# A two-layer decoder trunk on one core: when the first heads' transposes, the bias tables and the sevens' weights take their turn

## The chip, the core and the metric

The kernel runs on one core of one Trainium2 chip. TensorE multiplies matrices; VectorE, ScalarE and GpSimd do the element-wise work, each in the order of its own queue; DMA engines move data between HBM and the on-chip memories. The profile calls these engines PE (and PEld for the loading of its stationary operand), DVE, ACT and POOL; SP issues most DMAs. The metric is the time of one execution on the device in microseconds.

## The reference

Two layers over 256 tokens of width 2048, in float32. Each layer:

```python
h = rmsnorm(x)
q, k, v, gate_b, gate_c, conv_in = split(h @ w_in)     # six parts of 1024 columns
q, k = rmsnorm of q and k per head half (64 wide), with gains
A = (softmax(q0 k0 + bias) - lam * softmax(q1 k1 + bias)) @ v     # 8 heads, causal
A = rmsnorm(A per head) * (1 - lam_init)
conv = gate_b * causal_conv3(gate_c * conv_in)
x = x + concat(A, conv) @ w_out
x = x + relu(rmsnorm(x) @ w_up) ** 2 @ w_down          # width 8192
```

The bias depends on the distance between two tokens alone: a table of 32 buckets by 16 half-heads is turned into rows by distance, and each row is read as a Toeplitz band.

## The kernel before

**Precision and weights.** Every float32 operand is split into a high half in TensorE's fp32r format and a low half that holds the rest; a product takes three matmuls (high by high, high by low, low by high). Weights come in as tiles `raw` of 512 KB, four buffers deep, through SP's queue. `Weights.halves` converts an ordinary tile: ScalarE writes the high half `whi` (L335), VectorE subtracts it to get the low half `wlo` (L336). These two have three buffers each, so a tile is converted as soon as TensorE is done with the tile three places ahead of it. `Weights.take` issues the conversions three tiles ahead.

**Sevens.** Some pairs of the inner dimension are multiplied by Strassen's scheme with seven products instead of eight (`BySeven`). Such a pair needs two raw tiles. Its job `plain` converts the left tile into `w7b` and a half of the right one into `whi` and `wlo` (ScalarE L844, VectorE L845); `sums` builds two differences on VectorE (L877, L878), converts them into `w7x`, and builds two more (L882, L883); `more` converts these into `w7y`. The activations' sums (`sv`, `sf`) are made by `sums_of`. In the first projection (`first`) query and key of heads 0 to 3 are accumulated with one such pair in layer 0 and two in layer 1. In `left`, the first half of the output projection, pairs by seven ("a" and "b", L902) alternate with columns of gate_b ("c", L426). A column accumulates in the one PSUM bank of tag `av`; `gate` copies it out on ScalarE (L798), multiplies it with the convolution on VectorE, and converts the result.

**Order of the work.** TensorE's instructions run in program order. The other engines' order is planned at compile time from the data that each instruction needs and a model of the durations; `late` holds an instruction at its place in the program. Work beside the projections is written as generators in a list (`Background`, `work`). After every six matmuls of a projection (one k tile of 128 rows by two token tiles by three terms) `work.tick()` advances each of them that is due: `yield n` means n ticks later. In `linear_t` a tick comes more often.

What runs there, in layer 0: `load_bias`, due at tick 10, first runs `small_setup`: a matmul makes the rows by distance (L250), VectorE copies them out, a DMA on POOL's queue writes them to DRAM (L252); four ticks later the gains and lambda are prepared. Then two DMAs on POOL's queue read the band tables `rev` of 1 MB each (L284), and 12 ticks later ScalarE copies them, reversed, into `bias` (L293, eight copies over four steps, each held `late`). `Norm.factors` sums the squares of the rows (tot, L575); `rstd_of` computes the factor on POOL (row_e, row_r; L494, L496); a matmul spreads it (rbc).

`qk_norm` starts when a half's query or key is complete: squares on ScalarE (L645), sums on VectorE, the power on POOL, and the scaled heads on VectorE (L653). 12 ticks later come the transposes of the first 128 tokens, four on TensorE (L662), and one tick later those of the other 128. Each group of four is put away by two copies on ScalarE and two subtractions on VectorE for queries (`qT`, L619 and L621), and by four copies and two subtractions for keys (`kT`, L631 and L632; `kL`, L634). In the first half queries and keys are normalised in place. With 16 ticks to a projection, the queries' transposes of the first half stand after the 10th and 11th step of v's projection, the keys' after the 12th and 13th.

`attention` starts one tick after v's projection in the first half and ten in the second. Its four heads start 8 ticks apart (16 in the second half): copies of the query (`both`, L681), two ticks on the scores (L691, L694), bias and maximum on VectorE (L699), exponentials on ScalarE (L708); ten ticks later the transposes (`ptp`, L724), four ticks later the product with v (L735, L737), its copy (`ao`, L740) and its squares (L743). After the last head the norm, 12 ticks, and the transposes `atp` (L767). After the two halves' projections follow gate_c and conv_in (`gc`, `ci`, L474), then `left` and `right`, then the MLP, which the change does not touch.

Of the kernel before, what the change touches and what calls it, by code (L numbers as in the profile page):

```python
# [131 lines left out]
def trunk(ctx: ExitStack, tc: tile.TileContext, x, w_in, w_out, conv_w, q_norm_g, k_norm_g,  # L132
# [114 lines left out]
    def small_setup(vec, lamv, sel, rel, prod, by_dist):  # L247
# [27 lines left out]

    def load_bias(l, bpool, biasp, bias, setup):

        if l == 0:
            yield from small_setup(*setup)
        revs = []  # L280
        for j in range(2):
            rev = bpool.tile([P, NH, S], F32, tag="b", name=f"rev{l}{j}")
            src = by_dist_d[j * NH:(j + 1) * NH, 0:S]
            nc.gpsimd.dma_start(  # L284
                rev, bass.AP(src.tensor, src.offset, [[1, P], [REL, NH], [1, S]]))
            revs.append(rev)
        yield 4 if l else 12
        while held:
            yield 1
        bias += [biasp.tile([P, NH, S], F32, tag="bias", name=f"bias{j}") for j in range(2)]  # L290
        for h in range(0, NH, 2):
            for j in range(2):
                late(nc.scalar.activation(bias[j][:, h:h + 2],  # L293
                                          revs[j][:, h:h + 2, ::-1], AF.Copy))
            yield 2
# [24 lines left out]
    class Weights:  # L320
# [8 lines left out]
        def halves(self, raw):  # L329
# [4 lines left out]
            if not self.by_tile:  # L334
                pair = (nc.scalar.activation(hi, raw, AF.Copy),  # L335
                        nc.vector.tensor_sub(lo, raw, hi.bitcast(F32)))  # L336
                if self.ramp and len(self.made) < 7:
                    for ins in pair:
                        late(ins)
# [151 lines left out]
    def rstd_of(ss, n, name, shape):  # L491
# [3 lines left out]
        r = small.tile([P, shape], F32, tag="rs_r", name=f"{name}_r")  # L495
        nc.gpsimd.tensor_tensor(r, e, mhalf[:, :shape], op=ALU.pow)  # L496
        return r

    class Norm:
# [3 lines left out]
        def __init__(self, which, l):  # L503
            self.which, self.l = which, l
            self.squared = 0
            self.tiles = [Parts(apool, "a", f"nT{which}{l}_{n}") for n in range(D // CH)]
# [64 lines left out]
        def factors(self):  # L571
# [3 lines left out]
            nc.vector.tensor_reduce(tot, self.ss, axis=AX.X, op=ALU.add)  # L575
            r = rstd_of(tot, D, "row", NT)
            self.r = small.tile([P, NT], F32, tag="rowf", name="rowf", bufs=2)
# [60 lines left out]

    def qk_norm(acc, r, put, gain, name, in_place=False):

        out_ = []
        for t in range(NT):
# [5 lines left out]
                                    axis=AX.X, op=ALU.add)  # L648
            f = rstd_of(ms, DK, f"{name}{t}", NH)
            f2 = small.tile([P, NH], F32, tag="f2", name=f"{name}f{t}")  # L650
# [6 lines left out]
            out_.append(qn)  # L657
        yield 12
        for t in range(NT):
# [3 lines left out]
            put(tp.rearrange("p (h c) -> p h c", c=P), gain, slice(t * P, (t + 1) * P))  # L663
            yield 1

    def attention(l, qT, kT, kL, v, h0, dst, bias, tmp, pace, sums_of):
# [9 lines left out]
        def unit(i):  # L676
# [72 lines left out]
            for _ in range(2):  # L749
                nc.gpsimd.tensor_tensor(flat, flat, rflat, op=ALU.mult)  # L750
            f = rstd_of(flat, P, f"a{h0}", 4 * NT)
            f2 = small.tile([P, 4, NT], F32, tag="af2", name=f"af2{h0}", bufs=2)
# [42 lines left out]
    def gate(c, acc, cv, dst, y):  # L795

        ev = nat.tile([P, 2, S], F32, tag="wide", name=f"gb{c}")
        nc.scalar.activation(ev, acc, AF.Copy)  # L798
        nc.vector.tensor_add(y, ev[:, 0], ev[:, 1])
# [4 lines left out]
        dst.ready = c % KG == KG - 1  # L804


# [3 lines left out]
    class BySeven:  # L810
# [3 lines left out]
        def __init__(self, l, bpool, biasp, tmp, weights, rooms_of=4):  # L814
            self.rooms_of = rooms_of
            self.l, self.pool, self.weights = l, bpool, weights
            self.biasp, self.tmp = biasp, tmp
            self.sums, self.rooms = {}, []

# [19 lines left out]
        def jobs(self, w, i, cols, in_keys=False):  # L839

            mine = {}

            def split(hi, lo, src):
# [12 lines left out]
            def plain():  # L856
# [9 lines left out]
                room = self.pool.tile([P, 2, 2, CH], F32R, tag="b", name="w7b")  # L866
                b11, b21 = two(room, raws[0])
                hi = wpool.tile([P, 2, CH], F32R, tag="hi", name="whi")
                lo = wpool.tile([P, 2, CH], F32R, tag="lo", name="wlo")
                return b11, b21, split(hi[:, 0], lo[:, 0], raws[1][:, 1])  # L870

            def sums():
# [3 lines left out]

                nc.vector.tensor_sub(t[:, 0], right[:, 0], left[:, 0])  # L877
                nc.vector.tensor_sub(t[:, 1], right[:, 1], right[:, 0])  # L878
                room = self.biasp.tile([P, 2, 2, CH], F32R, tag="bias", name="w7x")
# [79 lines left out]
        def left(self, acts, cv):  # L959
# [8 lines left out]
            def column(c):  # L968
# [161 lines left out]
    def mixer(l, norm, loads):  # L1130

        with ExitStack() as scope:
# [24 lines left out]
            bias = []  # L1157
            work.start(load_bias(l, bpool, biasp, bias, setup), 20 if l else 10)
            hT = norm.tiles
# [5 lines left out]
            for half in range(2):  # L1165
# [19 lines left out]
                for t in range(NT):  # L1185
# [516 lines left out]
```

## Time and profile before

| | us |
|---|---|
| median of three runs (lowest, highest) | 2119.78 (2117.97, 2120.92) |
| the profiled execution | 2118.42 |
| its span, first to last instruction | 2116.6 |
| busy in the span: TensorE | 2107.7 |
| VectorE | 1817.5 |
| ScalarE | 1402.7 |
| POOL | 161.5 |

The granted clock of TensorE is 1.000 of full speed over the span. In a row of the timeline or of the chain of waits the first number is the start in microseconds from the span's first instruction, the second the duration; then engine, line, operation, output <- inputs, shapes and count; in brackets stands the idle time of the engine before the instruction and what ended it. In a row of waits stand the total, the number of times and the longest. A matmul's own duration overlaps its neighbours'; the distance between starts is what it costs.

### The profile page before, as it was taken

Reading aid. Unit: us, or ns where it says so; the run is one execution under the profiler, and the core shown is the slowest. Engines: PE = TensorE matmul, PEld = TensorE weight load, DVE = VectorE, ACT = ScalarE, POOL = GpSimd, SP = SyncE. Lnnn points to the kernel's source line nnn. Section 1 sums busy time; section 2 is a strip of 40 time slices with the busy share of each in tenths; the row PEclk is TensorE's granted clock in tenths of the full one; section 3 lists DMA queues with packets and bytes.
Section 4 is the critical chain, followed back from the end, with each engine's and each line's share of the span. In section 5 each row is a group of like instructions: output and inputs, shape, how many; then the busy total and the mean of one; then the engine's idle time right before and its main releaser. Section 6 shows DMA issues by size and latency. Waiting matters only on the chain.

```text
span 2116.6 us, 29201 instructions
## 1 busy us (share of the span) xinstructions
PE 2107.7 (100%) x10815; PEld 1800.4 (85%) x10815; DVE 1817.5 (86%) x2497; ACT 1402.7 (66%) x1817; POOL 161.5 (8%) x226
## 2 busy tenths in 40 slices
PE   9999999999999999999999999999999999999999
PEld 7888888888888888888888888888888888888887
DVE  7778788898888888799887788888988888888998
ACT  6777656676666676666567766557677677675664
POOL 2110100000000000011102101000000000000110
PEclk9999999999999999999999999999999999999999
DMA  7555565877777777789565555658877777777993
GB/s 272 178 159 172 179 207 189 288 253 225 234 232 230 233 232 230 247 298 311 171 219 170 163 174 181 200 180 295 259 230 234 231 231 235 230 231 256 318 309 111
DMA packets 312608, 476.01 MB, mean 225 GB/s; under 512 B 12724, under 2 KB 209670, under 8 KB 312465
## 3 DMA queue, kind: packets, MB, share of 16 engines
q1 hardware_dynamic: 284752, 406.76, 60.5%
q0 software_dynamic: 27520, 67.24, 10.1%
q8 instruction: 85, 1.39, 0.3%
q14 instruction: 59, 0.48, 0.1%
q10 hardware_dynamic: 192, 0.15, 0.0%
HBM read 440.52 MB, written 33.58 MB: 224 GB/s over the span
## 4 chain that ended last, share of the span: by engine, by line
PE 97%; ACT 1%; DMA 1%; DVE 1%; issue 0%; POOL 0%; ACTq 0%; DVEq 0%; POOLq 0%
PE upc L1376 31%; PE pr L1419 14%; PE dn L1500 8%; PE ci L474 4%; PE gc L474 4%; PE gb L426 4%; PE v L449 3%; PE o L919 3%; PE dn L1419 3%; PE k L449 2%; PE po L902 2%; PE q L449 2%; PE dn L1594 2%; PE pr1r L1419 2%; PE pr0r L1419 2%; PE po L919 2%
## 5 line engine op out<-in xcount | busy, mean ns | idle before, releaser
L1376 PE MATMUL upc<-nT,uhi 128*128 128x512 f32 x1920 | 454.7, 389 | 0.0
L1376 PEld LDWEIGHTS upc<-nT,uhi 128*128 128x128 f32 x1920 | 360.3, 188 | 74.7
L1241 DVE TENSOR_TENSOR ulo<-uraw,uhi 128x1024 fp32r<-128x1024 f32 x256 | 312.2, 1222 | 109.6 <-ACT f L1408 91.5
L335 ACT ACTIVATE whi<-raw 128x1024 fp32r<-128x1024 f32 x236 | 249.2, 1059 | 191.1 <-issue 20.6
L1240 ACT ACTIVATE uhi<-uraw 128x1024 fp32r<-128x1024 f32 x256 | 270.6, 1057 | 135.2 <-PE upc L1376 114.9
L336 DVE TENSOR_TENSOR wlo<-raw,whi 128x1024 fp32r<-128x1024 f32 x236 | 285.8, 1221 | 85.1 <-ACT whi L335 52.7
L1376 PEld LDWEIGHTS upc<-nT,ulo 128*128 128x128 f32 x1920 | 246.2, 191 | 9.4
L1376 PE MATMUL upc<-nT,ulo 128*128 128x256 f32 x1920 | 249.1, 283 | 0.0
L1266 ACT ACTIVATE bh<-draw 128x1536 fp32r<-128x1536 f32 x86 | 128.4, 1493 | 103.7 <-PE pr L1419 80.7
L1267 DVE TENSOR_TENSOR bl<-draw,bh 128x1536 fp32r<-128x1536 f32 x86 | 151.3, 1759 | 11.5 <-ACT bh L1266 11.0
L1500 PE MATMUL dn<-whi,fb 128*128 128x512 f32 x480 | 152.2, 389 | 0.0
L1419 PE MATMUL pr<-bh,f 128*128 128x512 f32 x360 | 121.4, 391 | 0.0
L335 ACT ACTIVATE whi<-uraw 128x1024 fp32r<-128x1024 f32 x60 | 63.7, 1062 | 71.9 <-PE dn L1500 55.1
L1386 ACT ACTIVATE ev<-upc 128x512 f32<-128x512 f32 x120 | 71.9, 599 | 54.2 <-PE upc L1376 54.2
L1266 ACT ACTIVATE t24h<-t 128x1024 fp32r<-128x1024 f32 x86 | 91.4, 1063 | 23.4 <-PE pr L1419 15.9
L1500 PEld LDWEIGHTS dn<-whi,fb 128*128 128x128 f32 x480 | 90.1, 188 | 18.8
L1267 DVE TENSOR_TENSOR t24l<-t,t24h 128x1024 fp32r<-128x1024 f32 x86 | 104.8, 1219 | 0.2
L1279 DVE TENSOR_TENSOR t<-draw 128x1024 f32<-128x1024 f32 x86 | 104.8, 1219 | 0.1
L1267 DVE TENSOR_TENSOR t13l<-t,t13h 128x1024 fp32r<-128x1024 f32 x86 | 104.8, 1219 | 0.0
L1266 ACT ACTIVATE t13h<-t 128x1024 fp32r<-128x1024 f32 x86 | 91.5, 1064 | 8.3 <-DVE t L1279 2.9
L1419 PE MATMUL pr<-t13h,f 128*128 128x512 f32 x240 | 93.8, 391 | 0.0
L1500 PE MATMUL dn<-wlo,fb 128*128 128x512 f32 x240 | 93.4, 389 | 0.0
(524 smaller groups left out, 4330.0 us busy)
## 6 DMA issues: line engine op xcount, KB each, us to landing
uraw<-in_w_up_dram SPq DMA_DIRECT2D x128, 1024.0 KB, 6.2
raw<-in_w_in_dram SPq DMA_DIRECT2D x191, 512.0 KB, 4.1
draw<-in_w_down_dram SPq DMA_DIRECT2D x180, 512.0 KB, 5.3
raw<-in_w_out_dram SPq DMA_DIRECT2D x64, 512.0 KB, 4.4
uraw<-in_w_down_dram SPq DMA_DIRECT2D x60, 512.0 KB, 6.6
hid0p<-f POOLq DMA_DIRECT2D x17, 512.0 KB, 3.5
fb<-hid0p POOLq DMA_DIRECT2D x17, 512.0 KB, 7.5
hid1p<-f POOLq DMA_DIRECT2D x17, 512.0 KB, 3.5
```

The source lines that it names most:

```text
L335: pair = (nc.scalar.activation(hi, raw, AF.Copy), nc.vector.tensor_sub(lo, raw, hi.bitcast(F32)))
L336: nc.vector.tensor_sub(lo, raw, hi.bitcast(F32)))
L449: nc.tensor.matmul(acc[:, t], a.ap[:, pa, k % KG, t * P:(t + 1) * P], (hi, lo)[pw][:, j], start=(k == 0 and (pa, pw) == (0, 0)), stop=(k = ...
L474: nc.tensor.matmul(acc[:, f, 0] if part else acc[:, f], wt[:, k % 4, fs], a.ap[:, 0, k % KG] if part else a.ap[:, :, k % KG], start=(part ...
L919: nc.tensor.matmul(accs[t], a.ap[:, pa, k % KG, t * P:(t + 1) * P], (hi, lo)[pw][:, j], start=(j == 0 and (pa, pw) == (0, 0) and (n, t) in ...
L1240: pair = (nc.scalar.activation(hi, src, AF.Copy), nc.vector.tensor_sub(lo, src, hi.bitcast(F32)))
L1241: nc.vector.tensor_sub(lo, src, hi.bitcast(F32)))
L1266: keep(nc.scalar.activation(hi, src, AF.Copy))
L1267: keep(nc.vector.tensor_sub(lo, src, hi.bitcast(F32)))
L1376: nc.tensor.matmul(acc[:, 0] if part else acc, wt[part][:, k], a.ap[:, 0, k % KG] if part else a.ap[:, :, k % KG], start=(part == 0 and kh ...
L1419: nc.tensor.matmul(prods[n], f[:, pa, a], b[pw], start=(start and m == 0), stop=(stop and m == 2))
L1500: nc.tensor.matmul(prods[p], f[:, pa, 2 * k + t], b[pw][:, n], start=(p in starts and k == 0 and m == 0), stop=(stop and k == 1 and m == 2))
```

## The change

It has three parts; no instruction that computes is added or taken away.

- *Bias tables.* The DMA that writes the rows by distance moves out of `small_setup` into `load_bias`. It is issued 8 ticks after the end of `small_setup`, once the row norm's power has been written into the program and no seven of the first projection is open, and `tc.issue_after` orders it behind that power on POOL's queue. The reads of the tables and, 12 ticks later, their copies move with it (from ticks 26 to 32 to ticks 35 to 41). In layer 1, nothing of this changes.
- *Transposes.* `qk_norm` takes its two delays as arguments. In the first half the queries wait 8 ticks instead of 12 and the keys 14; the two groups of each are 3 ticks apart instead of 1. They now stand after v's 6th and 9th step, and after its 14th and one step into the next projection. The first half's attention starts 4 ticks after v instead of 1; the second half's start is kept at 10.
- *Sevens.* `tc.issue_after(x)` orders, on the engine of x, each instruction of its block behind x. In `left`, the conversions of `plain` and the two differences of `sums` are ordered behind the last ordinary tile's conversion (ScalarE and VectorE) and the last gate copy (ScalarE) that precede them in the program. In the first projection this holds for the two differences alone, behind the last ordinary tile's low half.

```diff
-        nc.gpsimd.dma_start(by_dist_d, by_dist)
...
-    def load_bias(l, bpool, biasp, bias, setup):
+    def load_bias(l, norm, bpool, biasp, bias, setup):
         if l == 0:
             yield from small_setup(*setup)
+            yield 8
+            while norm.powered is None or held:
+                yield 1
+            with tc.issue_after(norm.powered.ins):
+                nc.gpsimd.dma_start(by_dist_d, setup[-1])
         revs = []
...
-    def qk_norm(acc, r, put, gain, name, in_place=False):
+    def qk_norm(acc, r, put, gain, name, in_place=False, wait=12, apart=1):
...
-        yield 12
+        yield wait
...
             put(tp.rearrange("p (h c) -> p h c", c=P), gain, slice(t * P, (t + 1) * P))
-            yield 1
+            yield apart
...
+            @contextmanager
+            def behind(ordered):
+                with ExitStack() as both:
+                    if ordered:
+                        for ins in self.weights.last + self.gated:
+                            both.enter_context(tc.issue_after(ins.ins))
+                    yield
...
-                b11, b21 = two(room, raws[0])
+                with behind(in_keys):
+                    b11, b21 = two(room, raws[0])
...
-                return b11, b21, split(hi[:, 0], lo[:, 0], raws[1][:, 1])
+                with behind(in_keys):
+                    b22 = split(hi[:, 0], lo[:, 0], raws[1][:, 1])
+                return b11, b21, b22
...
-                nc.vector.tensor_sub(t[:, 0], right[:, 0], left[:, 0])
-                nc.vector.tensor_sub(t[:, 1], right[:, 1], right[:, 0])
+                with behind(in_keys or self.rooms_of == 8):
+                    nc.vector.tensor_sub(t[:, 0], right[:, 0], left[:, 0])
+                    nc.vector.tensor_sub(t[:, 1], right[:, 1], right[:, 0])
...
-                gate(c, acc, cv, self.cat[2 + c // KG], y[:, c % 2])
+                self.gated = gate(c, acc, cv, self.cat[2 + c // KG], y[:, c % 2])
...
                     work.start(qk_norm(acc, norm.r, put, gain[:, l:l + 1], "qk"[n] + f"{l}{half}",
-                                       half == 0))
+                                       half == 0, *(((8, 3), (14, 3))[n] if half == 0 else (12, 1))))
...
                 work.start(attention(l, qT, kT, kL, v, h0, cat[half], bias[half], tmp,
-                                     1 + half, by_seven.sums_of), 1 + 9 * half)
+                                     1 + half, by_seven.sums_of), 4 + 6 * half)
```

The other lines of the diff set what these use: `Weights.last` is the last ordinary tile's pair of conversions, `gate` returns its copy, `rstd_of` returns its power, `Norm.powered` keeps it.

More of the change, by code (lines that the diff above doesn't have):

```diff
@@ L1 @@
 import math
-from contextlib import ExitStack
+from contextlib import ExitStack, contextmanager
 import concourse.bass as bass
@@ L336, in halves @@
                         nc.vector.tensor_sub(lo, raw, hi.bitcast(F32)))
+                self.last = pair
                 if self.ramp and len(self.made) < 7:
@@ L1157, in mixer @@
             bias = []
-            work.start(load_bias(l, bpool, biasp, bias, setup), 20 if l else 10)
+            work.start(load_bias(l, norm, bpool, biasp, bias, setup), 20 if l else 10)
             hT = norm.tiles
```

17 lines of the change are left out of this document (9 added, 8 removed).

## The prediction

> **What bounds the kernel now.** I read the first section of the page, then TensorE's own waits, then the timeline and the chain of waits around each of them. The execution that was profiled took 2118.42 us, 1.8 us of them outside its span.
>
> ```profile
> span 2116.6 us, 29201 instructions
> PE 2107.7 (100%) x10815; PEld 1800.4 (85%) x10815; DVE 1817.5 (86%) x2497; ACT 1402.7 (66%) x1817; POOL 161.5 (8%) x226
> ```
>
> TensorE is busy for all but 8.9 us, and the change removes no matmul. So it can win only what TensorE now loses in stalls. Its waits name them:
>
> ```profile
> PE q L449 <- DVE wlo L336: 2.1, 2, 1.1
> ...
> PE k L919 <- DVE wlo L336: 0.7, 1, 0.7
> ...
> PE po0r L902 <- DVE w7y L845: 0.3, 1, 0.3
> PE gb L426 <- ACT gb L798: 0.2, 1, 0.2
> ```
>
> Idle time understates a stall, because the pipeline has to fill again. The timeline of TensorE shows by how much, and shows one stall that has no idle time:
>
> ```profile
> 35.98 0.39 PE L919 MATMUL k<-whi,nT 128*128 128x512 f32 x1
> 37.07 0.50 PE L919 MATMUL k<-wlo,nT 128*128 128x512 f32 x1 [0.70 <-DVE wlo L336]
> 37.41 0.62 PE L919 MATMUL k<-whi,nT 128*128 128x512 f32 x2
> ...
> 39.70 1.17 PE L902 MATMUL po0r<-w7b,nT 128*128 128x512 f32 x3
> 40.71 0.86 PE L902 MATMUL q<-w7b,nT 128*128 128x512 f32 x3
> ```
>
> ```profile
> 56.60 12.24 PE v L449 x54
> ```
>
> Undisturbed, a matmul follows the last after 12.24 / 54 = 0.227 us, and six of them, one **step** of the background work, take 1.36 us. In the first fence the starts are 1.09 and 0.34 apart: 0.86 + 0.11 = 0.97 us lost for 0.70 shown, so 0.27 more than is shown. The three matmuls from 39.70 take 1.01 instead of 0.68: 0.33 lost, none of it shown. With 0.27 added to each wait, the stalls that the change can reach are 0.97 and 0.33 and 0.3 + 0.27 = 0.57 in the first projection of layer 0; 2.1 + 2 x 0.27 = 2.64 in the second half's query projection, one stall in each layer; 0.2 + 0.27 = 0.47 in a gate column. **Sum 4.98 us, 0.235%.** This is the most that the change can win; a measurement of this kernel tells about 0.2%, 4.2 us, from no change.
>
> **Part 1, the bias tables and the first product by seven.** The chain of waits there:
>
> ```profile
> 26.41 8.07 DMA raw<-in_w_in_dram
> ...
> 35.20 0.69 DVE w7t L878
> 35.88 1.14 DVE wlo L336
> ...
> 42.02 0.73 POOL row_r L496
> ```
>
> ```profile
> 34.59 0.69 DVE L877 TENSOR_TENSOR w7t<-raw 128x512 f32<-128x512 f32 x1 [3.71 <-DMA raw<-in_w_in_dram]
> ```
>
> ```profile
> L336 DVE TENSOR_TENSOR wlo<-raw,whi 128x1024 fp32r<-128x1024 f32 x236 | 285.8, 1221 | 85.1 <-ACT whi L335 52.7
> ...
> raw<-in_w_in_dram SPq DMA_DIRECT2D x191, 512.0 KB, 4.1
> ```
>
> ```profile
> 26.52 1.81 POOL L284 DMA_DIRECT2D rev<-by_dist_d  x2 [1.62 <-DMA by_dist_d<-setup]
> ```
>
> A load that takes 4.1 us elsewhere took 8.07, because both table reads of 1 MB were issued 0.1 us behind it. VectorE sat 3.71 us in front of two subtractions that need this load, while the ordinary tile's low half (35.88) stood behind them in its queue. The change removes both causes. The low half now goes first, into the idle 3.71 us that begin at 30.9; it needs 1.22 us and ends by 33 instead of 37.0, so the 0.97 stall goes. The load lands about 4 us earlier, at 30.5, so the subtractions follow at once, and VectorE's chain to the last parts of the seven (two adds of 0.69, three subtractions of 1.22) runs some 2 us sooner: it was late by 0.33 and 0.57. Nothing is added but order. I take all 1.87 us; if the row norm on POOL holds the last part, 0.57 stays.
>
> What the moved step issues: a small write and two reads on POOL's queue, now behind the pow at 42.02, so near 43 to 45. POOL's next work behind them is the query norm, after the projection has ended. Their readers and their new neighbours:
>
> ```profile
> rev<-by_dist_d POOLq DMA_DIRECT2D x2, 1024.0 KB, 10.0
> ```
>
> ```profile
> 51.20 1.06 ACT L335 ACTIVATE whi<-raw 128x1024 fp32r<-128x1024 f32 x1 [1.65 <-PE k L919]
> 52.16 1.14 ACT L293 ACTIVATE bias<-rev 128x512 f32<-128x512 f32 x2
> ```
>
> The reads take 10.0 us and land by 56. The copies of the tables, eight on ScalarE in pairs of 1.14 us, move from around v's start to its 5th to 11th step, from 56.6 + 5 x 1.36 - 1.9 = 61.5 on: over 5 us of cover. The Trainium skill, page "DMA: Bandwidth & Descriptors", Rules for kernel authors, says the reverse of this edit: issue a DMA early and wait late. In the trace the early issue cost 4 us on a load that TensorE needed, so here the row speaks against the rule; what the rule would make of the time is a rival below. The loads that the reads now meet are those of v's weights. The conversion at 51.20 waited for TensorE, not for its load; from it to v's first matmul (56.60) are 5.4 us, less 1.06 and 1.22 of conversion 3.1: its lead. A load that doubles as the one at 26.41 did is 4 us late. The loads are issued some 2 us sooner, as the sevens' buffers are returned sooner, so I take 0; bounds 0 and 1.
>
> ScalarE's room for the moved copies (the columns of busy time are PE, PEld, DVE, ACT, POOL):
>
> ```profile
> 62.00:86.00 24.00, 22.94 (x110) 18.67 (x109) 18.67 (x25) 18.11 (x24) 5.63 (x6) 1.00 0.50 151
> ```
>
> It is busy for 18.1 of these 24 us; three pairs move in, 3.4 us. It fits, and nearly fills it.
>
> **Part 2, the transposes.** ScalarE in front of the stall in layer 0:
>
> ```profile
> 74.79 1.04 ACT L335 ACTIVATE whi<-raw 128x1024 fp32r<-128x1024 f32 x1
> ...
> 76.30 0.68 ACT L631 ACTIVATE kT<-k00tp,gains 64x512 fp32r<-64x512 f32 x1
> ...
> 81.18 0.69 ACT L632 ACTIVATE kT<-k00tp,gains 64x512 fp32r<-64x512 f32 x1
> 81.89 2.01 ACT L335 ACTIVATE whi<-raw 128x1024 fp32r<-128x1024 f32 x2
> ```
>
> The eight copies of the keys stand in a row, 5.6 us, and the weight conversions are 7.1 us apart where TensorE eats a tile in 2.72; VectorE waits with them. That is the 1.3 us stall of each layer. Now the queries come after v's 6th and 9th step, the keys after the 14th and one step into the next projection: four copies (2.8 us) per three steps (4.1), with one or two conversions of 1.05 between. The longest row without a conversion is v's two evictions (taken like two copies) and four copies, 1.4 + 2.8 = 4.2; it begins right behind a conversion, so the next, due 2.72 later, is 1.5 late of a lead of 3.1. So both stalls go: 2.64 us, bounds 1.3 and 2.64. The transposes are as many as before. The queries are asked for four steps sooner and must be normalised by then:
>
> ```profile
> 1113.90 0.69 DVE L653 TENSOR_TENSOR qe<-qe,q10f 128x512 f32<-128x512 f32 x1
> ```
>
> ```profile
> 1107.99 13.66 PE v L449 x60
> ```
>
> In layer 1, the tighter one, done at 1114.6; v's 6th step ends near 1108 + 8.2 = 1116.2: some 1.5 us of cover.
>
> The first half's attention starts three steps later. Its four heads keep their spacing, but their last product now falls on the step of the second half's first key transposes. There the trace has the same row of eight copies, and the smallest lead that TensorE survives:
>
> ```profile
> 156.58 0.69 ACT L632 ACTIVATE kT<-k01tp,gains 64x512 fp32r<-64x512 f32 x1
> 157.29 1.06 ACT L335 ACTIVATE whi<-raw 128x1024 fp32r<-128x1024 f32 x1
> ```
>
> ```profile
> 156.88 3.34 PE L474 MATMUL gc<-nT,whi 128*128 128x512 f32 x14
> ```
>
> ```profile
> 146.51 0.38 ACT L740 ACTIVATE ao<-av 128x256 f32<-128x256 f32 x1 [0.89 <-PE av L737]
> 147.39 0.31 ACT L743 ACTIVATE s<-ao 128x128 f32<-128x128 f32 x1 [0.49 <-DVE ao L741]
> 147.61 0.19 ACT L743 ACTIVATION_READ_ACCUMULATOR s<-ao 128x1 f32 x1
> ```
>
> The tile converted at 157.29 to 158.35 is wanted eight matmuls into gc, at 156.88 + 1.81 = 158.69: 0.34 us to spare. The product brings a copy of 0.38 and two squares of about 0.5, 1.4 us, into this row. All in front of the conversion: 1.4 - 0.34 = 1.06 us lost in each layer. None, if the conversion, whose buffer is free long before, is ordered ahead of two of the copies. In the nearest row all eight went ahead, which speaks for the loss; a fuller ScalarE speaks for the conversion. I take half, 0.55 a layer, **1.1 us given back**; bounds 0 and 2.1.
>
> **Part 3, the sevens' weights in the gate columns.**
>
> ```profile
> 1335.96 0.86 PE L902 MATMUL po<-w7x,sf 128*128 128x512 f32 x3
> ```
>
> ```profile
> 1334.52 1.06 ACT L844 ACTIVATE w7b<-raw 128x1024 fp32r<-128x1024 f32 x1 [3.47 <-DMA raw<-in_w_out_dram]
> ...
> 1337.78 0.58 ACT L798 ACTIVATE gb<-gb 128x512 f32<-128x512 f32 x1
> ```
>
> ScalarE sat 3.47 us in front of a seven's conversion whose load was late; behind it stood an ordinary tile and the gate copy that frees the one PSUM bank of the next column. Put in front, the copy starts when its column ends, near 1336 (the product behind it starts at 1335.96), and the 0.47 goes. New waits: the seven's first conversions now stand behind the ordinary tile's, whose buffer TensorE frees at the column's end. Their own product comes nine matmuls and a column later, at least 25 x 0.227 = 5.7 us; they need 1.06 and a half-size conversion on ScalarE, and two of 0.69, one of 1.22 and a half-size one on VectorE, 3.2: covered. Bounds 0 and 0.47; I take 0.4.
>
> **Sum**: 1.87 + 2.64 + 0.4 - 1.1 = 3.8 us. The profiled execution becomes 2114.6. It lies 1.36 under the median of 2119.78; against that median the forecast is **2116.0 us**, 0.18% faster, at the edge of what can be told.
>
> **The rivals.**
> *The key row gives everything back*: 2.1 instead of 1.1, 2117.0. For it: the order of the eight copies.
> *The planner keeps the rows*: the other engines' order is planned, and the spread may only shift the row of copies; then the 2.64 stay and 3.8 becomes 1.2: 2118.6. Against it: three steps lie between the transposes.
> *Slower: the table reads starve v's loads.* The Trainium skill, same page, "Issuing engines are not separate DMA queues", says that DMAs of all issuers share the same engines and interleave; the 8.07 us agrees. Place: layer 0, 45 to 57 us. It decides when a load of v's weights takes over 4.1 + 3.1 + 2 = 9.2 us. If they take as long as both reads need (10.0 plus the 0.9 between the issues, and 4.1 of their own, 15.0), TensorE waits 5.8 us, the net is 2.0 us slower: 2121.8. Against it: 8.07 is what a load under both reads took.
> *Late tables*: the copies are held in program order, so a late read stops ScalarE's conversions behind it. With 5 us of cover and 3.1 of lead the reads must take over 18 us instead of 10; at 24 us TensorE waits 6 us: 2122.0. The Trainium skill's rule on early issue, told above, points this way.
>
> **How the numbers follow.** Forecast (gain 2.8 to 5.0) 58%; key row 12%; rows kept 14%; starved loads 9%; late tables 3%; other new stalls on a nearly full VectorE 4%. Over 0.2% faster needs a gain of 4.2, the forecast with little given back: 35%. Slower by over 0.2% needs over 8 us of new stalls: half of the starved and late cases, where they are worse than priced, and the other new stalls: 10%. The rest, 55%, within. The range goes from the full 4.98 with 1 us of run spread, 2113.8, to just over no gain, 2121.0.
>
> **What would show it.** Right: no TensorE wait on wlo in either second-half q; VectorE's 3.71 us gap shorter and the low half ahead of it; the seven's second load near 4 us; the reads after row_r, landed before the first table copy; the gate copy ahead of the seven's conversion. Wrong: a new wait at the start of gc in both layers, v's matmuls waiting for wlo near 55 us, or transposes that wait for the query norm.

## The result and the profile after

The changed kernel takes **2113.65 us** (median of 11 runs, 2113.47 to 2113.88); the kernel before took 2118.67 in the same comparison (11 runs, 2117.96 to 2120.92). The ratio is **0.9975, 95% interval 0.9965 to 0.9984**: 5.0 us faster. The forecast was 2116.0, its range began at 2113.8. That is the whole of the 4.98 us that the prediction called the most that could be won, though it had booked 1.1 us of them as given back; so the question is where the gain came from. The spread is news too: 0.4 us after, 3.0 us before.

The page of the changed kernel, then all that TensorE waits for in it (total, times, longest):

```profile
span 2112.0 us, 29197 instructions
...
PE 2107.1 (100%) x10815; PEld 1801.5 (85%) x10815; DVE 1815.9 (86%) x2497; ACT 1401.5 (66%) x1817; POOL 181.0 (9%) x226
```

```profile
PE warm L187 <- DVE mhalf L179: 1.1, 1, 1.1
PE tpb L568 <- DMA x<-in_x_dram: 0.2, 1, 0.2
```

The span is 4.6 us shorter and TensorE's work the same. Every wait for wlo, w7y and the gate copy is gone from the list; the two that are left belong to the kernel's start.

**First product by seven.** VectorE's timeline of the changed kernel:

```profile
31.37 1.23 DVE L340 TENSOR_TENSOR wlo<-raw,whi 128x1024 fp32r<-128x1024 f32 x1 [0.35 <-ACT whi L339]
32.51 0.69 DVE L895 TENSOR_TENSOR w7t<-raw 128x512 f32<-128x512 f32 x1
```

The low half now stands ahead of the differences, and the gap of 3.71 us is 0.35. The seven's second load, issued at 26.56 with nothing beside it, takes (last column, from issue to landing):

```profile
raw<-in_w_in_dram SPq DMA_DIRECT2D x1, 512.0 KB, 4.5
```

The table reads now meet two loads of v's weights, issued between 43.5 and 46 us (the row of rev is the second read; the first took 8.9):

```profile
rev<-by_dist_d POOLq DMA_DIRECT2D x1, 1024.0 KB, 11.8
raw<-in_w_in_dram SPq DMA_DIRECT2D x2, 512.0 KB, 10.3
```

They take 10.3 instead of 4.1 us, and TensorE does not wait.

One stall of the prediction's three stays. Before w7y stands the row norm in VectorE's queue, and TensorE spends 1.05 us on three matmuls (42.25 to 43.30) that need 0.68. VectorE, then TensorE:

```profile
39.84 0.17 DVE L583 COPY rowf<-row_r 128x2 f32<-128x2 f32 x1 [0.62 <-POOL row_r L501]
39.92 1.23 DVE L340 TENSOR_TENSOR wlo<-raw,whi 128x1024 fp32r<-128x1024 f32 x1
...
41.45 1.22 DVE L859 TENSOR_TENSOR w7y<-w7t,w7y 128x1024 fp32r<-128x1024 f32 x1
```

```profile
42.25 1.21 PE L920 MATMUL po0r<-w7y,sf 128*128 128x512 f32 x3
43.30 0.85 PE L920 MATMUL q<-w7y,nT 128*128 128x512 f32 x3
```

1.05 - 0.68 = 0.37 us are lost without idle time.

**The transposes.** ScalarE in front of the old stall at 84.7:

```profile
76.61 0.69 ACT L636 ACTIVATE kT<-k00tp,gains 64x512 fp32r<-64x512 f32 x1
...
79.41 1.06 ACT L339 ACTIVATE whi<-raw 128x1024 fp32r<-128x1024 f32 x1
...
81.08 0.67 ACT L636 ACTIVATE kT<-k00tp,gains 64x512 fp32r<-64x512 f32 x1
...
83.88 1.06 ACT L339 ACTIVATE whi<-raw 128x1024 fp32r<-128x1024 f32 x1
```

Four key copies, a conversion, four copies, a conversion: the row of eight is cut in two and the stall is gone in both layers.

**The key row of the second half**, where the first half's last product now falls. ScalarE, then TensorE:

```profile
147.00 1.06 ACT L339 ACTIVATE whi<-raw 128x1024 fp32r<-128x1024 f32 x1 [1.61 <-PE v L454]
147.96 0.37 ACT L745 ACTIVATE ao<-av 128x256 f32<-128x256 f32 x1
148.22 0.67 ACT L636 ACTIVATE kT<-k01tp,gains 64x512 fp32r<-64x512 f32 x1
...
151.00 0.31 ACT L748 ACTIVATE s<-ao 128x128 f32<-128x128 f32 x1
...
154.52 2.01 ACT L339 ACTIVATE whi<-raw 128x1024 fp32r<-128x1024 f32 x2
```

```profile
153.85 3.88 PE L479 MATMUL gc<-nT,whi 128*128 128x512 f32 x16
```

What was feared has come: the copy and the squares stand among the eight key copies, all in front of the conversion. From the conversion ahead of the row to the one behind it are 154.52 - 147.00 = 7.52 us, where before had 157.29 - 150.75 = 6.54: 0.98 longer, not 1.4, since neighbours overlap. And the need comes later too, since the product's six matmuls lie between: TensorE wants the tile eight matmuls into gc, at 155.67, 8.67 behind the row's first conversion, where before wanted it 7.94 behind. The spare 0.34 shrinks by 0.98 - 0.73 to 0.09. The high half is written at 155.58, its loading as TensorE's stationary operand (0.19 us on PEld) waits 0.23 us for it and starts at 155.63, and TensorE loses 0.1 us. Layer 1 shows the same.

**The gate columns.** The gate copy goes first, the seven's conversion behind it, its load long there:

```profile
1332.23 0.60 ACT L803 ACTIVATE gb<-gb 128x512 f32<-128x512 f32 x1 [1.57 <-PE gb L431]
1332.73 1.06 ACT L858 ACTIVATE w7b<-raw 128x1024 fp32r<-128x1024 f32 x1
```

### The profile page after: what moved, and what is told of

The parts are those of the page before. It is cut to its first block, busy times and chain, and to the rows that moved or that the text cites. A ratio compares the mean times of both kernels' runs of the same rounds, so it can differ in the third digit from the quotient of the medians.

```text
span 2112.0 us, 29197 instructions
## 1 busy us (share of the span) xinstructions
PE 2107.1 (100%) x10815; PEld 1801.5 (85%) x10815; DVE 1815.9 (86%) x2497; ACT 1401.5 (66%) x1817; POOL 181.0 (9%) x226
## 4 chain that ended last, share of the span: by engine, by line
PE 99%; DMA 0%; DVE 0%; ACT 0%; issue 0%; DVEq 0%
PE upc L1394 31%; PE pr L1437 14%; PE dn L1518 8%; PE gc L479 4%; PE ci L479 4%; PE gb L431 4%; PE v L454 4%; PE o L937 3%; PE dn L1437 3%; PE po L920 2%; PE k L454 2%; PE q L454 2%; PE dn L1612 2%; PE pr1r L1437 2%; PE pr0r L1437 2%; PE q L937 2%
```

## The experiments

Theory: each part removes stalls of TensorE, and their sizes add. Rivals: the stalls are not constants, or the parts depend on one another. All medians; each ratio is to the kernel before on the same chip. The comparisons were made on different chips, and the median of before moves by 0.8 us between them, so a difference of that size between two rows says little by itself.

| kernel | us | runs from, to | ratio, 95% interval |
|---|---|---|---|
| before, five comparisons | 2118.67 to 2119.46 | 2116.43, 2121.32 | |
| changed | 2113.65 | 2113.47, 2113.88 | 0.9975 (0.9965 to 0.9984) |
| part 1 alone | 2121.39 | 2118.86, 2125.14 | 1.0011 (1.0002 to 1.0019) |
| part 2 alone | 2117.04 | 2115.13, 2118.38 | 0.9991 (0.9983 to 1.0000) |
| part 3 alone | 2117.31 | 2114.84, 2118.45 | 0.9993 (0.9983 to 1.0002) |
| without part 1 | 2114.78 | 2113.55, 2115.62 | 0.9978 (0.9968 to 0.9987) |
| without part 2 | 2119.72 | 2117.53, 2121.55 | 1.0002 (0.9993 to 1.0010) |
| without part 3 | 2115.51 | 2114.76, 2117.37 | 0.9981 (0.9972 to 0.9989) |
| order alone | 2119.67 | 2117.59, 2121.95 | 1.0003 (0.9994 to 1.0012) |
| old reads, new order | 2115.03 | 2113.34, 2117.39 | 0.9980 (0.9971 to 0.9988) |
| moved reads, old order | 2113.78 | 2113.01, 2114.05 | 0.9975 (0.9966 to 0.9984) |
| attention at once | 2117.93 | 2117.71, 2120.90 | 1.0000 (0.9992 to 1.0009) |
| attention at three | 2114.41 | 2114.02, 2114.64 | 0.9975 (0.9965 to 0.9985) |
| norm behind the seven | 2113.48 | 2113.06, 2114.81 | 0.9976 (0.9965 to 0.9986) |
| reads doubled | 2118.65 | 2116.71, 2120.53 | 0.9996 (0.9987 to 1.0005) |

### Part 1 alone

Edit to the kernel before:

```diff
+            with tc.issue_after(norm.powered.ins):
+                nc.gpsimd.dma_start(by_dist_d, setup[-1])
...
+                with behind(self.rooms_of == 8):
```

> The kernel before with the first part of the change alone (table reads behind the row norm; the two differences behind the low half). Theory A, the parts add up and each is worth the TensorE stalls that it removes: the stalls at 37.07 (0.97 us) and 40.14 (0.33 us) go, of the one at 44.13 (0.57 us) the 0.36 us stay that the changed kernel still shows there; 1.5 us, so 2116.9 in the profiled execution against 2118.42, and both 2.1 us waits of q for wlo stay. Theory B, the early reads also delay the loads of x at the start: 0.6 us more, 2116.3, and the 0.59 us stall near 6.9 us is gone as well. Theory C, the reads under v's loads cost something that the other parts hide: less than 1.0 us gained, with new waits of v for wlo between 45 and 60 us.

None of the three held: 2121.39, 0.11% **slower** than before, by an interval that just excludes no change. TensorE's timeline, and ScalarE's:

```profile
83.79 0.49 PE L454 MATMUL q<-whi,nT 128*128 128x512 f32 x1 [1.62 <-ACT whi L339]
85.51 0.79 PE L454 MATMUL q<-wlo,nT 128*128 128x512 f32 x1 [1.23 <-DVE wlo L340]
```

```profile
71.42 2.78 ACT L624 ACTIVATE qT<-q00tp,q_gain 64x512 fp32r<-64x512 f32 x4
74.22 1.06 ACT L339 ACTIVATE whi<-raw 128x1024 fp32r<-128x1024 f32 x1
75.19 1.14 ACT L297 ACTIVATE bias<-rev 128x512 f32<-128x512 f32 x2
...
82.68 2.00 ACT L339 ACTIVATE whi<-raw 128x1024 fp32r<-128x1024 f32 x2
```

The last table copies and the query copies now lie directly in front of the row of eight key copies: no conversion between 75.3 and 82.7 us, and where before lost 1.33 us two waits of 1.62 and 1.23 follow each other. TensorE then runs at half clock (window, length, busy time of PE, PEld, DVE, ACT, POOL, granted clock, DMA share, GB/s):

```profile
86.00:88.00 2.00, 2.00 (x6) 1.52 (x6) 1.97 (x3) 0.93 (x2) 0.00 (x0) 0.50 0.69 166
```

So the parts depend on one another: ScalarE has no room for the moved copies until the transposes are spread.

### Part 2 alone

```diff
+                                       half == 0, *(((8, 3), (14, 3))[n] if half == 0 else (12, 1))))
...
+                                     1 + half, by_seven.sums_of), 4 + 6 * half)
```

> The kernel before with the second part alone (first half's transposes spread, first half's attention started three steps later). Theory A: both waits of q for wlo go (2.64 us), and each layer loses 0.1 us at the start of gc: 2.4 us gained, 2116.0 in the profiled execution. Theory B, the row of eight key copies gives back 0.55 us a layer, as the prediction had it: 1.5 us gained, 2116.9. Theory C, the spread needs the later bias copies to fit on ScalarE: a wait of q for wlo of about 1 us stays in layer 0 only, 2117.0.

2117.04; its profiled execution took 2115.22. Both waits of q are gone, as theory A has it. But so, in this execution, were all three stalls of the first seven, which the edit does not touch: the load at 26.31 took 6.1 us instead of 8.1. The gate columns' waits, not touched either, were 0.6 instead of 0.2. That was the first sign that the stalls behind loads are not constants; the size of part 2 can't be read from this run alone.

### Part 3 alone, and the changed kernel without it

```diff
+                with behind(in_keys):
```

> The kernel before with the third part alone (sevens' weights behind the ordinary tile and the gate copy in the gate columns). Theory A: the stall of 0.47 us at 1338.4 goes and nothing else moves: 2117.95 in the profiled execution. Theory B, the order only moves the wait to the seven's own product: 2118.4 with a wait of po for w7b or w7x of 0.2 us or more in its place.

> The changed kernel without its third part (the sevens' weights in the gate columns in the planner's own order). Theory A, the wait of the gate columns is as long as the seven's load is late in that execution (0.47 us before, 0.17 + 0.49 + 0.45 us with the second part alone, 0.38 + 0.99 + 0.30 us with the first alone): median 0.5 to 1.5 us above the changed kernel's 2113.65, so 2114.1 to 2115.2, and runs that spread by over 1 us where those of the changed kernel spread by 0.4. Theory B, a fixed stall of 0.47 us: 2114.1 and no more spread than the changed kernel has.

Alone 2117.31: the stall is gone and none takes its place, and the median falls by more than the 0.47 us of the profile, though the interval still holds no change. Without part 3 the median is 2115.51, so that by the medians the part is worth 1.9 us in the changed kernel, above both theories' guess of the size; the spread of 2.6 us speaks for A. Its waits (total, times, longest) and ScalarE:

```profile
PE gb L431 <- ACT gb L803: 1.2, 3, 0.5
```

```profile
1331.87 1.06 ACT L858 ACTIVATE w7b<-raw 128x1024 fp32r<-128x1024 f32 x1 [3.73 <-DMA raw<-in_w_out_dram]
...
1335.13 0.57 ACT L803 ACTIVATE gb<-gb 128x512 f32<-128x512 f32 x1
```

Three waits, with 0.27 each for the pipeline 1.2 + 0.81 = 2.0 us, where before's profile had one of 0.47.

### The changed kernel without part 1, and its two halves

```diff
+        nc.gpsimd.dma_start(by_dist_d, by_dist)
...
-            with tc.issue_after(norm.powered.ins):
-                nc.gpsimd.dma_start(by_dist_d, setup[-1])
...
-                with behind(in_keys or self.rooms_of == 8):
+                with behind(in_keys):
```

> The changed kernel without its first part (tables read early, the two differences ahead of the low half). Theory A, the stalls of the first product by seven are there only in executions in which the load beside the table reads lands late (8.1 us in the profile of before, 6.0 us in that of the second part alone, where TensorE did not wait at all): median between 2113.7 and 2115.3, spread over about 2 us. Theory B, they are there each time: 2115.2 with a spread of 0.4. Theory C, the first part buys nothing once the others are in: 2113.6 and no spread.

2114.78, from 2113.55 to 2115.62: theory A. Now the halves: the order alone on the kernel before (the second of the two lines of part 1); the changed kernel with the early reads; and the changed kernel without the order.

> The kernel before with one line of the first part: the two differences of the first seven ordered behind the low half; the tables are read at their old place. Theory A, what made the first part alone slower is the move of the tables, not this order: the wait of k for wlo near 37 us (0.97 us) goes and nothing comes in its place, 0.5 to 1 us below before, 2117.5 to 2118.5. Theory B, any new order on VectorE lets the planner come out elsewhere and the waits near 84 us grow as with the first part alone: 2120 or more.

> The changed kernel with the table reads at their old, early place, and the two differences still behind the low half. Theory A, the order alone takes away the wait of k for wlo (0.97 us in before), whatever the load does, and the load's lateness still reaches the seven's last parts (0.33 and 0.57 us): 2113.7 to 2114.5. Theory B, the late load is the whole cause and the order does nothing: as without the first part, 2114 to 2115.3, with the wait of k for wlo near 37 us when the load is late. In both, the copies of the tables on ScalarE are back near 50 us.

> The changed kernel with the table reads at their new, late place, and the two differences of the first seven left where the planner puts them. Theory A, the reads' place is the whole of the first part: the load lands in about 4.5 us each time, the differences follow it whichever order is asked for, and the time is the changed kernel's, 2113.5 to 2113.9 with a spread of about 0.4 us. Theory B, both halves are needed: without the order the low half stands behind the differences and k waits for wlo near 37 us by up to 0.97 us: 2114.2 to 2114.9.

The order alone gives 2119.67, no change. Its profile shows why; VectorE, and TensorE's wait:

```profile
31.19 1.23 DVE L336 TENSOR_TENSOR wlo<-raw,whi 128x1024 fp32r<-128x1024 f32 x1 [0.36 <-ACT whi L335]
34.10 0.69 DVE L891 TENSOR_TENSOR w7t<-raw 128x512 f32<-128x512 f32 x1 [1.68 <-DMA raw<-in_w_in_dram]
```

```profile
PE po0r L916 <- DVE w7y L855: 1.6, 1, 1.6
```

The low half is early and k no longer waits, but the load is late all the same (7.6 us), and the whole lateness comes out at w7y: 1.6 + 0.27 = 1.87 us. That this equals the three stalls of the first profile is in part chance, for the load took 8.1 there. The gate columns waited 2.4 us in this execution, in five waits, more than in any other profile. With the early reads in the changed kernel the runs go from 2113.34 to 2117.39; with the late reads and no order they are at 2113.78, like the changed kernel. So theory A of the last run holds: **the place of the reads is the whole of part 1**. In the profile without the order the 0.37 us at 42.7 are gone as well: w7y stands ahead of the low half there, at 39.76 instead of 41.45. So with the order of the two differences the stall is left, and without it it is not; the medians do not tell the two kernels apart.

### The changed kernel without part 2

```diff
-                                       half == 0, *(((8, 3), (14, 3))[n] if half == 0 else (12, 1))))
+                                       half == 0))
...
-                                     1 + half, by_seven.sums_of), 4 + 6 * half)
+                                     1 + half, by_seven.sums_of), 1 + 9 * half)
```

> The changed kernel without its second part (first half's transposes and attention as before; table reads moved, sevens ordered). Theory A, the moved table copies need the room on ScalarE that the spread transposes make: as with the first part alone the conversions of the second half's first tiles come after eight key copies and are later still, some 4 us lost near 84 us where before lost 1.3, and 1.3 in layer 1; 2118 to 2120. Theory B, the loss of the first part alone (2121.4) was that of its gate columns, which the third part mends: 2.64 us above the changed kernel, 2116.3, with two stalls of 1.3 us.

2119.72: theory A, with the same pair of waits near 84 us (1.7 and 1.2) and the half clock behind them. Part 2 is worth 6.1 us beside the others, not 2.64.

### The start of the first half's attention

```diff
-                                     1 + half, by_seven.sums_of), 4 + 6 * half)
+                                     1 + half, by_seven.sums_of), 1 + 9 * half)
```

> The changed kernel with the first half's attention started one step after v, as in the kernel before. Theory A, the moved product costs 0.1 us in each layer, since its six matmuls (0.69 us) lie in front of gc and put off the need for the next tile by nearly as much as its copies (0.94 us) lengthen ScalarE's row: the two stalls of 0.1 us at the start of gc go, 0.2 us faster than the changed kernel, 2113.7 in a profiled execution against 2113.88. Theory B, the prediction's price of 0.55 us a layer: 2112.8. Theory C, the later start is needed, because the heads' copies otherwise meet the spread key transposes: waits of q for wlo come back, 1 us or more in each layer, 2115.9 or more.

2117.93. Theory C's size, by another way: not q waits for wlo, but the scores for the keys (the waits, then TensorE in a second execution):

```profile
PE sc L696 <- DVE kL L639: 4.0, 2, 2.0
```

```profile
1137.24 0.47 PE L696 MATMUL sc<-kL,both 128*128 128x512 f32 x1 [2.00 <-DVE kL L639]
```

The later start, which the prediction booked as a cost, is what makes the spread possible. With three steps (`3 + 7 * half`):

> The changed kernel with the first half's attention started one step sooner (three steps after v instead of four; second half unchanged), so that its last product leaves the step of the second half's first key transposes. Theory A, the key row costs 0.1 us in each layer: both stalls at the start of gc go, and the scores, now near 85.8 us, still find the keys written (83.9 us): 0.2 us faster, 2113.45. Theory B, the prediction's price of 0.55 us a layer is paid somewhere in the changed kernel: 2112.6. Theory C, the scores have to wait for the keys' second half, as they did for 2.16 us in each layer with the start at one step: 2114 or more, with a wait of sc for kL.

```profile
PE q11tp L667 <- DVE mx L704: 0.3, 1, 0.3
PE q01tp L667 <- DVE mx L704: 0.3, 1, 0.3
```

2114.41. Both stalls at the start of gc are gone, as A said, but the heads now meet the second half's query transposes, which wait for the maximum of the scores in both layers. Of the starts 1, 3 and 4, one is the worst by over 3 us. Between three and four the profiles speak for four (spans of 2112.8 and 2112.0 us, with waits of 0.6 us that four does not have), but the ratios to before are the same, 0.9975.

### The rest of the w7y stall

```diff
+            with ExitStack() as order:
+                if not self.which and self.l == 0:
+                    while not self.sevens.closed:
+                        yield 1
+                    order.enter_context(tc.issue_after(self.sevens.closed.ins))
+                nc.vector.tensor_copy(self.r, r)
```

`closed` is the low half of w7y.

> The changed kernel with one more order: in layer 0 VectorE copies the row norm's factor (rowf) only behind the low half of the seven's last parts (w7y), so that its wait for POOL no longer stands in front of them. Theory A, the 0.36 us that TensorE still loses at 42.7 us is that wait, passed on by VectorE's queue: it goes, 2113.3. Theory B, the last parts are late by their own chain (differences, conversions) and the stall stays: 2113.65. Theory C, rowf now comes too late for the query norm or the spread sum: new waits of 0.3 us or more, 2114 or above.

```profile
39.86 1.22 DVE L864 TENSOR_TENSOR w7y<-w7t,w7y 128x1024 fp32r<-128x1024 f32 x1
41.00 0.16 DVE L588 COPY rowf<-row_r 128x2 f32<-128x2 f32 x1
```

w7y is 1.6 us sooner and TensorE's stall is gone: theory A for the cause. The median is 2113.48 of 8 runs, 0.2 below the changed kernel, but the runs overlap and the ratio is the same: no better version by this measure.

### The table reads twice

```diff
+            if l == 0:
+                spare = nc.dram_tensor(f"spare{j}", [P, NH, S], F32, kind="Internal").ap()
+                nc.gpsimd.dma_start(
+                    spare, bass.AP(src.tensor, src.offset, [[1, P], [REL, NH], [1, S]]))
```

> The changed kernel with each table read done twice, the second time into a spare piece of DRAM that nobody reads (2 MB more from layer 0's table, at the same place on POOL's queue). Theory A, v's loads share the DMA engines with the reads: they took 10.1 and 10.6 us under two reads and can take some 11.6 before TensorE waits (the tile used at 57.59 has 1.47 us to spare); under four they take 15 to 20 us, and TensorE waits 4 to 8 us for v's weights between 55 and 62 us: 2117.5 to 2122. Theory B, the loads' queue gets its share whatever the number of reads: loads of 10 to 12 us, under 1 us lost, 2113.6 to 2114.6.

2118.65, in theory A's range, but only in part by theory A's way. Loads issued from 43 to 52 us, TensorE's waits, and VectorE:

```profile
raw<-in_w_in_dram SPq DMA_DIRECT2D x4, 512.0 KB, 13.5
```

```profile
PE v L458 <- DVE wlo L344: 3.5, 2, 3.0
```

```profile
65.05 0.23 DVE L660 TENSOR_SCALAR k00f<-k_r,rowf 128x8 f32<-128x8 f32 x1 [1.53 <-POOL k_r L505]
...
65.92 2.36 DVE L344 TENSOR_TENSOR wlo<-raw,whi 128x1024 fp32r<-128x1024 f32 x2
```

The loads share with the reads: these four take 13.5 us, where the changed kernel's four took 8.8 and cost nothing. But the longer of the two waits, 3.0 us, is that of a low half (65.92) that stands behind the key norm in VectorE's order. Its high half was written at 63.36; VectorE then sat until 65.05 for the keys' power, which POOL reaches only after the two powers of the queries (62.93 to 65.01). The changed kernel waits for the same power, 1.67 us until 64.73, but there the planned order has the low half ahead, at 61.71. By an estimate from these rows, ahead of the norm it would have ended at 63.36 + 1.22 = 64.58 and TensorE, idle from 64.24, would have waited some 0.4 us. So of the 3.5 us of waits the loads account for about 0.9, and the other order for the rest.

### Two more executions of the kernel before, and of the early attention

> The kernel before, unchanged, in another execution. Theory A, the stalls that the change removes in the first product by seven and in the gate columns are drawn anew in each execution, by how late a load lands: the sum of the stalls at 37 to 45 us (1.87 us in the first profile) and of those in the gate columns (0.49 us there) differs by 0.5 us or more from it, and the two stalls near 84.7 and 1135.7 us (1.33 each) stay to 0.1 us. Theory B, the order of the queues fixes them: all of them stay to 0.1 us.

> As the look before it: theory A says that the stalls behind loads (37 to 45 us, gate columns) come out otherwise again, by 0.5 us or more, with the seven's second load between 4 and 9 us; theory B that they are those of the first profile to 0.1 us.

TensorE's waits in the two executions of the unchanged kernel before, which took 2119.78 and 2117.17:

```profile
PE q L449 <- DVE wlo L336: 2.1, 2, 1.1
...
PE k L919 <- DVE wlo L336: 1.0, 2, 0.7
PE gb L426 <- ACT gb L798: 0.6, 2, 0.4
...
PE po0r L902 <- DVE w7y L845: 0.3, 1, 0.3
```

```profile
PE q L449 <- DVE wlo L336: 2.1, 2, 1.1
...
PE gb L426 <- ACT gb L798: 0.7, 2, 0.4
```

Theory A, though not at each place in each execution. The load beside the reads took 8.1 us in the first, where the first seven lost 1.9 us as in the first profile, and 4.4 in the second, where it lost nothing. The gate columns lost 0.6 + 0.54 = 1.14 and 0.7 + 0.54 = 1.24 us instead of 0.47, and in the first of the two a second wait of k for wlo came up, in layer 1 at 1084.9 us. Only the two waits of q are the same in all three.

> The changed kernel with the first half's attention one step after v, in another execution. Its eleven times fell into 2117.7 to 2117.9 and 2119.0 to 2119.3. Theory A, the two groups are executions without and with a stretch of half clock (granted 0.50, seven matmuls 0.20 us longer each) behind one of the two waits of 2.16 us: near 2117.8 without such a stretch, near 2119.1 with one, 2120.7 with two. Theory B, the half clock always follows the wait at 85 us and the groups differ by late loads: a stretch of half clock at 86 to 89 us whichever the time.

> As the look before it: theory A says a time near 2117.8 goes with no stretch of half clock and one near 2119.1 with one; theory B says half clock at 86 to 89 us each time.

The times were 2120.96 and 2119.42. In the second, the granted clock (third number from the end) around its two equal waits:

```profile
84.00:86.00 2.00, 0.64 (x4) 0.62 (x5) 1.96 (x7) 1.56 (x3) 0.00 (x0) 1.00 0.48 185
86.00:88.00 2.00, 2.00 (x11) 1.64 (x10) 2.00 (x5) 1.18 (x3) 0.00 (x0) 1.00 0.05 4
...
1138.00:1140.00 2.00, 2.00 (x8) 1.57 (x7) 2.00 (x5) 0.74 (x3) 0.00 (x0) 0.67 0.19 17
1140.00:1142.00 2.00, 2.00 (x6) 1.61 (x5) 1.35 (x4) 2.00 (x7) 0.00 (x0) 0.50 0.74 243
```

Full clock behind the first, half clock behind the second; the other execution had it behind both and took 1.5 us more; the first profile had it behind the first alone, at 2119.17. Theory A, as far as it was seen: no execution near 2117.8, the group without such a stretch, was profiled.

## Why the prediction came out as it did

The direction was right, and so was the main mechanism of each part. The gain was put 1.2 us too low, and the chance of over 0.2% faster at 35%.

- **The step that failed: "This is the most that the change can win."** The 4.98 us were read from one execution and taken as fixed, and the fast end of the range was built on them. Half of them are fixed (the waits of q); the others stand behind loads and come out anew in each execution. In the three profiled executions of before they came to 1.87 + 0.47, 1.9 + 0.5 + 1.14 and 0 + 0.25 + 1.24 us (the middle terms are layer 1's k, read from the distances between starts). With the 2.64 the second lost 6.2 us at the places that the change reaches, more than "the most", and the third 4.1. Less the 0.37 and 0.2 us that stay in the changed kernel, the three should be 4.4, 5.6 and 3.6 us slower than its profiled execution; they were 4.5, 5.9 and 3.3. The mean, 4.5, leaves 0.5 of the 5.0 us of the medians open.
- **The key row was mis-sized**: 1.1 us given back in the sum, with 2.1 as the worst case; 0.2 measured, 0.9 of the 1.2 us that the forecast gain lacked, though all eight copies did stay in front. The working added durations that overlap (1.4 for 0.98) and forgot that the product's own matmuls put off the need by 0.73.
- **Part 3 was mis-sized**: 0.4 us taken, 0.47 as its bound; 0.47, 1.14 and 1.24 in the three executions, and 1.9 by the medians with and without it. The mechanism, a gate copy held up by a late seven, was right.
- **Part 1**: 1.87 us taken, the 0.57 us named as what the row norm may keep; 0.37 of them stay, for that reason. By the medians it is worth 1.1, since the stall does not come in each execution. This term was too high where the two above were too low, and that they partly cancel is luck. The cause named second, the order of the queue, is none: it alone gains nothing. That the reads would land by 56 us was right (55.3).
- **Part 2**: 2.64 us for the waits of q is right to 0.1. The prediction took ScalarE's room from the busy share of a window (18.1 + 3.4 of 24 us) part by part; part 1 without part 2 is slower than before, so the room was not there until the transposes were spread. Against the kernel before on their chip the parts alone gain -2.5, 1.9 and 1.6 us, 1.0 together, where the whole gains 5.0: the sizes do not add. The later start was priced as a cost; without it the spread loses 2.16 us in each layer.
- **The rivals.** Starved loads did not come, and the point of decision was too low: loads of 10.3 us, above the 9.2, cost nothing, since the low half of the tile used at 57.6 still ended 1.47 us ahead of its matmul. The late tables and the kept rows did not come.
- **The anchor**: the profiled execution was 1.36 us below the median of three and was moved up to it. The median of 11 lies 0.25 above the profiled execution, so of the 2.35 us between the forecast time and the measured one 1.1 is the three runs' own spread; against the profiled executions the gain was 2118.42 - 2113.88 = 4.5 for a forecast of 3.8.

## What to carry to other kernels

A stall behind a load is a draw: compare several executions before calling it a size, and judge an edit that takes a late load off a queue by the spread that it removes. Room on a queue is read from its longest row without the urgent instruction, not from its busy share, and two edits that fill and empty the same row are to be priced together. When work is moved ahead of a deadline, its instructions on the waiting engine move the deadline too.

## What the runs showed of the hardware

- **A wait of 2 us may cost 3.6.** By the distance between starts the wait itself cost 2.16 us. Behind four of the six waits of 2.0 us in the three profiles of the early attention, and behind 1.62 and 1.23 us close together in both profiles that had them, TensorE's granted clock was then 0.50 for some 3 us: the matmuls follow each other in 0.427 instead of 0.227 us, seven or eight of them, 1.5 us more. A wait of 3.0 us with the reads doubled had a clock of 1.00 behind it; the waits of 1.1 us never had less. The Trainium skill, page "TensorE: Matmul & The Clock Gate", section "What's actually happening", puts the gate down to a free-running activity window of about 3.4 us and asks for a whole idle one. That the drop comes by chance agrees with a free-running window; that 2.0 us were enough does not agree with a whole idle one.
- **A load beside two reads of 1 MB is not slowed by a fixed factor.** In the eight profiled executions with the early reads the seven's second load took 4.4, 5.2, 6.1, 6.7, 7.6, 8.1, 8.1 and 8.2 us, where it took 4.5 with nothing beside it. The first read was issued 0.08 to 0.33 us behind it, and that does not decide: it was 0.23 us for the 4.4 and the 5.2, and 0.24 for the 8.2. What does is open.
